# Twelve names in other places of a hand-written attention schedule

## The chip, the cores and the metric

The kernel runs on one core of a Trainium2 chip. The metric is the device time of one execution in microseconds. The tensors are fp32; matrix products are made of three matmuls on split operands (a high part, rounded to the matmul's input format, and a low part, the rest).

## The reference

Two transformer layers over 1024 tokens of width 1024, each a token mixer and a gated MLP with a causal depthwise convolution. Layer 0's mixer, the part that the change touches, is differential attention: 8 heads, each with two sets of queries and keys of 64 columns, one value of 128 columns, and a chunk-causal mask.

```python
def diff_attention(h, w_qkv, ..., subln_g, w_o, lambda_init, cos, sin):
    qkv = h @ w_qkv
    ...                                  # rotary on the first 16 of 64 columns of q and k
    def block(args):                     # 128 queries at a time
        sc = jnp.einsum('bqhcd,bkhcd->bhcqk', qb, k).astype(jnp.float32) * scale
        p = masked_softmax(sc, chunk_mask(blk, s)[None, None, None])
        a = p[:, :, 0] - lam * p[:, :, 1]
        return jnp.einsum('bhqk,bkhe->bqhe', a.astype(v.dtype), v)
    ...
    o = rms_norm(o, subln_g) * (1.0 - lambda_init)
    return o.reshape(b, s, D_MODEL) @ w_o
```

Layer 1 (multi-head latent attention) and the two MLPs are as large in time, but nothing of theirs changes.

## The kernel before, in words

Layer 0's attention is cut into 32 steps: 8 heads with 4 steps each, step p of a head (p = 0 to 3) for the query blocks 2p and 2p+1 of 128 tokens, with the keys up to there. A step is a bundle of small named parts (`DaStep`), and each part issues one or a few instructions on one engine. Beside the steps run the projections of what comes next: `units` gives each step one or two of them (U, V), again in named parts.

The order of all this is written out by hand. `DA_SCORE` has four rows, one for each p; row t mod 4 is read when step t is current. A name without a mark belongs to step t, each `'` means one step earlier, each `+` one later. `da_steps` reads a row from left to right and calls the parts; a name of a step or a part that does not exist is skipped. The engines TensorE, VectorE, ScalarE and GpSimd run what they are given in exactly this order, each in its own queue; two names on different engines are ordered only by their data, by buffers that come free, and by nothing in the row. The DMA queue of SP is not under the manual order. Row t = 1 is replaced by `DA_SECOND`, and the last four steps (t = 28 and on) by `DA_END`.

The names, with the engine and the line by which the profile shows them:

- S0, S1: scores of the step's two blocks (TensorE, 1914 and 1915). M0, M1: mask and row maximum (VectorE, 1924 and 1925; 1928 and 1929 for p above 1, where a and b mark the two components). E0a, E0b, E1a, E1b: exponentials (ScalarE, 1940).
- I0, I1: inverse of the row sums (VectorE, 1945 and 1946). C0, C1: scaling of the first component by it (line 149 on GpSimd for p below 2, line 147 on ScalarE else). X0, X1: the mixing, first component plus a negative multiple of the second (VectorE, 1953).
- T0 to T3: transposes of the mixed probabilities (TensorE, 1961), three or four of 128x128 each. H0 to H3: high part (ScalarE, 127). L0 to L3: low part (VectorE, 130). A0 to A3: product with the values (TensorE, 119 to 121). O: copy of the product (ScalarE, 1989).
- Q1, Q2 (ScalarE, 1995 and 1998), Q3 (GpSimd, 130), F (TensorE, 2006 and 2007), R1 to R3 (ScalarE, 2013 to 2017), N1 to N3 (VectorE, 2022 to 2026): squares, their sum, and the head's normalisation, ending in a store. They exist for odd p.
- U0, U1, V0, V1: the two halves of a projection, 12 matmuls each (TensorE, 119 to 121, into the one bank `u`). Us, Um (VectorE, 657 and 661) and Up, Ua (GpSimd, 689): rotary. Uka to Ukd: keys, where a and c are casts of ScalarE (672) and b and d low parts of VectorE (670). Uqa to Uqf: queries, where a, b, d, e are casts of ScalarE (127) and c and f low parts of GpSimd (130). Vc, Vt, Vh, Vl: values (ScalarE 640, TensorE 645, ScalarE 127, VectorE 130).
- Wh, Wl: high and low part of the next head's weights, 128x1024 (ScalarE, 127; GpSimd, 130). Wl also starts the load of the next weights.

Step 3 of a head keeps TensorE busy into the next head: its probabilities are transposed and multiplied in rows 0 and 1 (T0', A0', then T3'', A1'', A2'', A3''), and the sum of squares F'' follows in row 1.

Of the kernel before, what the change touches and what calls it, by code (L numbers as in the profile page):

```python
# [56 lines left out]
class Trunk:  # L57
# [234 lines left out]
    def steps(self, attend, units, prepare, n, apart=False):  # L292
# [32 lines left out]


    DA_SCORE = (
# [4 lines left out]
    )  # L332

    DA_SECOND = "S0 I1' Vc' Ukd' H2'' M0 L2'' A1'' C0' X0' H3'' E0b L3'' U0 A2'' E0a Wh Vt' N3'''' A3'' O'' Wl' Q2'' C1' I0 X1' U1 C0 S1 X0 Us Vh' Q1'' T0' H0' Q3'' Up F'' Um M1 Ua Wl R1'' Vl' E1b V0 E1a L0' I1 A0' Uqa R2'' R3'' Uqd Uqe Uqb C1 X1 N1'' Uqc V1 T1 T0 Uqf H0"

    DA_END = (
# [9 lines left out]
    def da_steps(self, attend, units, prepare, n, extra):  # L346
# [4 lines left out]
        with self.tc.manual_schedule(engines={E.PE, E.DVE, E.Activation, E.Pool}):  # L351
            for t in range(-1, first + len(self.DA_END)):
                while len(steps) < min(n, t + 2):
# [3 lines left out]
                    for name, u in zip("UV", units(x)):  # L357
                        steps[x].parts.update({name + part: f for part, f in u.items()})
                row = self.DA_SECOND if t == 1 else self.DA_SCORE[t % 4] if t < first else self.DA_END[t - first]
                for name in row.split():  # L360
# [2004 lines left out]
```

## Time and profile before

| what | value |
|---|---|
| runs, median (lowest to highest) | 2399.78 us (2396.99 to 2400.72) |
| profiled execution | 2396.82 us, its span 2395.0 us |
| TensorE matmul busy | 2348.3 us (98%) |
| VectorE busy | 1947.0 us (81%) |
| ScalarE busy | 1292.0 us (54%) |
| GpSimd busy | 613.6 us (26%) |
| mean granted TensorE clock | 0.998 |
| layer 0's attention in rows and ending | about 48 us to 480 us |

The span is the time from the first to the last instruction. Busy shares are means over stages with different limits; what a change in one stage is worth is read from that stage: which engine TensorE waits for there, and what that engine was waiting for. Times in the timeline count from the start of the span.

### The profile page before, as it was taken

What the parts mean: (1) busy time and instruction counts of PE and PEld (TensorE: products, weight loads), DVE (VectorE), ACT (ScalarE), POOL (GpSimd) and SP (SyncE); (2) the same over time, 40 slices, a digit from 0 to 9 for tenths busy, and PEclk for the clock granted to TensorE, in tenths of its full rate; (3) what the DMA queues carried; (4) which work ended last, traced back from release to release, by engine and by line L of the source; (5) the groups of instructions that cost most, each with busy time, mean ns of one, the idle gap of its engine ahead of it and who ended that gap; (6) DMA issues with size and microseconds to landing.
All of it is one profiled execution on the core that took longest, in us unless ns stands there. A gap on an engine that the chain in (4) does not pass through costs nothing.

```text
span 2395.0 us, 32652 instructions
## 1 busy us (share of the span) xinstructions
PE 2348.3 (98%) x11952; PEld 1995.3 (83%) x11952; DVE 1947.0 (81%) x3185; ACT 1292.0 (54%) x2367; POOL 613.6 (26%) x484
## 2 busy tenths in 40 slices
PE   8999999999999999999999999999999999999998
PEld 7888888888888888888898789988888888887886
DVE  7888888858888888999864788886488888889997
ACT  5677767745444444443445777775354444444544
POOL 4555555424000000000132666664320000000001
PEclk9999999999999999999999999999999999999999
DMA  3111111333222222643222111123322222227502
GB/s 146 40 36 36 36 49 54 111 101 115 80 86 91 80 80 83 229 167 99 82 91 64 60 41 41 41 87 114 107 79 83 92 81 79 82 86 281 176 1 79
DMA packets 95664, 213.39 MB, mean 89 GB/s; under 512 B 8712, under 2 KB 33936, under 8 KB 95504
## 3 DMA queue, kind: packets, MB, share of 16 engines
q1 hardware_dynamic: 86304, 183.51, 23.0%
q10 hardware_dynamic: 9200, 27.80, 3.1%
q8 instruction: 94, 1.54, 0.3%
q14 instruction: 66, 0.54, 0.1%
HBM read 158.85 MB, written 52.43 MB: 88 GB/s over the span
## 4 chain that ended last, share of the span: by engine, by line
PE 85%; DVE 6%; ACT 3%; issue 2%; DMA 2%; POOL 2%; SPq 0%; POOLq 0%; DVEq 0%; ACTq 0%
PE S L119 13%; PE S L121 13%; PE S L120 13%; PE b L119 8%; PE b L120 8%; PE b L121 8%; PE u L119 4%; PE u L121 4%; PE u L120 4%; PE b L263 2%; PE u L2071 1%; PE u L2070 1%; PE S L1915 1%; PE S L1914 1%; PE b L1961 1%
## 5 line engine op out<-in xcount | busy, mean ns | idle before, releaser
L167 POOL TENSOR_TENSOR st<-st,mhalf 128x1 f32<-128x1 f32 x56 | 36.2, 647 | 1307.9 <-DVE st L164 1300.0
L119 PE MATMUL S<-s,u 128*128 128x512 f32 (+1 forms) x800 | 302.1, 378 | 2.5 <-DVE s L130 2.1
L121 PE MATMUL S<-s,u 128*128 128x512 f32 (+1 forms) x800 | 301.1, 376 | 0.4 <-DVE u L130 0.4
L120 PE MATMUL S<-s,u 128*128 128x512 f32 (+1 forms) x800 | 301.0, 376 | 0.0
L127 ACT CAST u<-h 128x512 fp32r<-128x512 f32 (+2 forms) x242 | 145.6, 619 | 273.3 <-DVE h L1082 271.6
L119 PE MATMUL b<-s,u 128*128 128x512 f32 x588 | 230.7, 392 | 1.8 <-DVE u L130 1.3
L121 PE MATMUL b<-s,u 128*128 128x512 f32 x588 | 229.0, 389 | 0.0
L120 PE MATMUL b<-s,u 128*128 128x512 f32 x588 | 229.0, 389 | 0.0
L1139 DVE SCALAR_TENSOR_TENSOR u<-u,conv,u 128x1023 f32<-128x1023 f32 (+1 forms) x176 | 224.9, 1278 | 0.8 <-ACT u L1135 0.7
L149 POOL TENSOR_TENSOR u<-u,st 128x512 f32<-128x512 f32 (+7 forms) x160 | 172.5, 1088 | 167.8 <-DVE st L2056 103.3
L127 ACT CAST s<-u 128x512 fp32r<-128x512 f32 (+3 forms) x230 | 145.4, 665 | 94.7 <-PE u L121 27.1
L119 PEld LDWEIGHTS S<-s,u 128*128 128x128 f32 x800 | 150.5, 188 | 30.9 <-DVE s L130 2.7
L130 DVE TENSOR_TENSOR u<-b,u 128x512 fp32r<-128x512 f32 (+1 forms) x256 | 158.6, 631 | 20.8 <-ACT u L127 18.2
L121 PEld LDWEIGHTS S<-s,u 128*128 128x128 f32 x800 | 150.5, 188 | 28.1 <-DVE u L130 0.6
L120 PEld LDWEIGHTS S<-s,u 128*128 128x128 f32 x800 | 150.5, 188 | 27.4
L127 ACT CAST u<-b 128x512 fp32r<-128x512 f32 (+1 forms) x256 | 134.9, 546 | 71.1 <-PE b L1961 39.7
L119 PE MATMUL u<-s,s 128*128 128x512 f32 (+1 forms) x408 | 162.4, 398 | 2.2 <-DVE s L130 1.3
L121 PE MATMUL u<-s,s 128*128 128x512 f32 (+1 forms) x408 | 157.9, 387 | 0.0
L120 PE MATMUL u<-s,s 128*128 128x512 f32 (+1 forms) x408 | 157.7, 387 | 0.0
L130 DVE TENSOR_TENSOR s<-u,s 128x512 fp32r<-128x512 f32 (+2 forms) x204 | 139.0, 715 | 11.8 <-ACT s L127 11.4
L1142 ACT ACTIVATE u<-u 128x1024 f32<-128x1024 f32 x44 | 46.7, 1062 | 186.5 <-DVE u L1139 186.4
L130 DVE TENSOR_TENSOR u<-h,u 128x512 fp32r<-128x512 f32 x171 | 117.4, 687 | 32.5 <-ACT u L127 31.5
(290 smaller groups left out, 6538.0 us busy)
## 6 DMA issues: line engine op xcount, KB each, us to landing
u<-in_ffn_up SPq DMA_DIRECT2D x88, 512.0 KB, 3.8
g_d<-u ACTq DMA_DIRECT2D x44, 512.0 KB, 2.6
u<-in_ffn_down SPq DMA_DIRECT2D x66, 256.0 KB, 4.7
u<-g_d SPq DMA_DIRECT2D x62, 256.0 KB, 4.2
s<-in_da_wqkv SPq DMA_DIRECT2D x23, 512.0 KB, 3.6
x_d<-u SPq DMA_DIRECT2D x16, 512.0 KB, 3.0
s<-x_d SPq DMA_DIRECT2D x8, 1024.0 KB, 10.4
u<-o_d SPq DMA_DIRECT2D x24, 256.0 KB, 2.9
```

Source lines behind the costliest of these rows:

```text
L119: mm(out, lh, rl, start=first, stop=False, skip_group_check=onto)
L120: mm(out, lh, rh, start=False, stop=False, skip_group_check=onto)
L121: mm(out, ll, rh, start=False, stop=last, skip_group_check=onto)
L127: self.nc.scalar.copy(out, src)
L130: (eng or self.nc.vector).tensor_sub(out, src, hi.bitcast(F32))
L149: self.nc.gpsimd.tensor_mul(x, x, s.to_broadcast(list(x.shape)))
L167: nc.gpsimd.tensor_tensor(r, s, self.mhalf, ALU.pow)
L263: self.nc.tensor.transpose(ps[:, j * P : (j + 1) * P], probs[t][:, k : k + P], self.ident)
L1139: nc.vector.scalar_tensor_tensor(t[half][:, back:], u[half][:, : S - back], w, t[half][:, back:], ALU.mult, ALU.add)
L1142: nc.scalar.activation(t[0], t[0], AF.Silu)
L1914: nc.tensor.matmul(sc[c][:, b : b + m], ql[c][:, qs], kt[:, c, :m], start=True, stop=False)
L1915: nc.tensor.matmul(sc[c][:, b : b + m], qh[:, c, qs], kt[:, c, :m], start=False, stop=True)
```

## The change

It is a change of four strings; no function changes, and no instruction is added or taken out. Moved are, in row 0: V0 behind R3''', T2' behind E0b, and T3' out of the row. In row 1 (and in `DA_SECOND`): T3'' near the front, Wh before U0, C1' before O'' (so before Wl'), X1' behind Wl', and Uqa behind R3''. In row 3: Uqb' before X1', and R1'' before I1.

```diff
     DA_SCORE = (
-        "S0 S1 M0 Up O'' R2''' V0 X1' R3''' N1''' M1 T1' Ua E0a H1' L1' Uka E1a T0' H0' T2' Ukb Ukc V1 E0b L0' I0 E1b A0' N2''' T3'",
-        "S0 I1' Vc' Ukd' H2'' M0 L2'' A1'' C0' X0' H3'' E0b L3'' U0 A2'' E0a Wh Vt' N3'''' A3'' O'' Wl' Q2'' C1' I0 X1' U1 C0 S1 X0 Us Vh' Wl Q1'' T0' H0' Q3'' Up F'' Um M1 Ua R1'' Vl' E1b V0 E1a L0' I1 A0' Uqa R2'' R3'' Uqd Uqe Uqb C1 X1 N1'' Uqc V1 T1 T0 Uqf H0",
+        "S0 S1 M0 Up O'' R2''' X1' R3''' V0 N1''' M1 T1' Ua E0a H1' L1' Uka E1a T0' H0' Ukb V1 Ukc E0b T2' L0' I0 E1b A0' N2'''",
+        "S0 I1' Vc' Ukd' T3'' H2'' M0 L2'' A1'' C0' X0' H3'' E0b L3'' Wh U0 A2'' E0a Vt' N3'''' A3'' C1' O'' Wl' X1' Q2'' I0 U1 C0 S1 X0 Us Vh' Wl Q1'' T0' H0' Q3'' Up F'' Um M1 Ua R1'' Vl' E1b V0 E1a L0' I1 A0' R2'' R3'' Uqa Uqd Uqe Uqb C1 X1 N1'' Uqc V1 T1 T0 Uqf H0",
         ...
-        "S0 U1 X1' Uqb' M0b T2' T0' Q2'' Q1'' ... Ul E1b I1 R1'' C1 +Um A2'",
+        "S0 U1 Uqb' X1' M0b T2' T0' Q2'' Q1'' ... Ul E1b R1'' I1 C1 +Um A2'",
     )
```

`DA_SECOND` gets the same edits as row 1.

More of the change, by code (lines that the diff above doesn't have):

```diff
@@ L327 @@
     DA_SCORE = (
[2 rows of a table removed]
[2 rows of a table added]
         "S0 Vm' O'' Vs' M0a L0' U0 Vp' Wh M0b E0a E0b Va' A0' I0 U1 N2''' H1' L1' Vka' Wl N3''' Vkc' Us Um C0 S1 M1b M1a E1b A1' E1a Vkd' Up +U0 Vkb' Ua I1 Uqa Uqd C1 Uqf Uqe O' X0",
[1 row of a table removed]
[1 row of a table added]
     )
-    DA_SECOND = "S0 I1' Vc' Ukd' H2'' M0 L2'' A1'' C0' X0' H3'' E0b L3'' U0 A2'' E0a Wh Vt' N3'''' A3'' O'' Wl' Q2'' C1' I0 X1' U1 C0 S1 X0 Us Vh' Q1'' T0' H0' Q3'' Up F'' Um M1 Ua Wl R1'' Vl' E1b V0 E1a L0' I1 A0' Uqa R2'' R3'' Uqd Uqe Uqb C1 X1 N1'' Uqc V1 T1 T0 Uqf H0"
+    DA_SECOND = "S0 I1' Vc' Ukd' T3'' H2'' M0 L2'' A1'' C0' X0' H3'' E0b L3'' Wh U0 A2'' E0a Vt' N3'''' A3'' C1' O'' Wl' X1' Q2'' I0 U1 C0 S1 X0 Us Vh' Q1'' T0' H0' Q3'' Up F'' Um M1 Ua Wl R1'' Vl' E1b V0 E1a L0' I1 A0' R2'' R3'' Uqa Uqd Uqe Uqb C1 X1 N1'' Uqc V1 T1 T0 Uqf H0"
     DA_END = (
```

2 rows, old and new, of the table DA_SCORE are left out of this document.

## The prediction

> **What bounds the kernel now.** I read the page first, for its chain of waits.
>
> ```profile
> PE 85%; DVE 6%; ACT 3%; issue 2%; DMA 2%; POOL 2%; SPq 0%; POOLq 0%; DVEq 0%; ACTq 0%
> ```
>
> TensorE carries 85% of the chain that ends last, so an edit to the order of names can only win the time in which TensorE stands still, or lose by making it stand longer. Next I read TensorE's waits, for the stretch in which the edited rows 0 and 1 run in their steady form (84 to 412 us, heads 1 to 6).
>
> ```profile
> PE b L2006 <- POOL h L130: 2.6, 6, 0.4
> PE b L119 <- DVE u L130: 1.9, 6, 0.4
> ```
>
> Two waits, once per head each, and no other: F'' (line 2006, released by GpSimd's Q3'') and A2'' (line 119, released by VectorE's L2''). Both stand in row 1. The first head's rows skip the names of steps that do not exist (no A2'', no F''), and the last head runs the untouched ending, so the change acts six times.
>
> The timeline of head 1 shows what the waits cost. Its columns are start, duration, instruction, and in brackets the idle time with its releaser. TensorE:
>
> ```profile
> 106.40 0.49 PE L1961 MATMUL b<-ident,u 128*128 128x128 f32 x3
> 106.65 0.42 PE L1914 MATMUL S<-u,h 128*128 128x384 f32 x1
> ...
> 110.43 0.39 PE L120 MATMUL u<-s,s 128*128 128x512 f32 x1
> 110.66 0.39 PE L121 MATMUL u<-s,s 128*128 128x512 f32 x1
> 111.41 0.39 PE L119 MATMUL b<-u,u 128*128 128x256 f32 x1 [0.36 <-DVE u L130]
> ...
> 117.04 0.49 PE L1961 MATMUL b<-ident,u 128*128 128x128 f32 x3
> 117.94 0.50 PE L2006 MATMUL b<-h,ones 128*128 128x512 f32 x1 [0.41 <-POOL h L130]
> ...
> 125.92 0.40 PE L1914 MATMUL S<-u,h 128*128 128x512 f32 x1
> ```
>
> The idle time in brackets is less than what is lost, as a matmul's reported end lies behind the next one's start. Matmuls of 512 columns follow each other after 0.23 (110.43 to 110.66), so A2'' was due at 110.89 and came at 111.41: 0.52 lost. Three transposes are followed by the next work after 0.25 (106.40 to 106.65), so F'' was due at 117.29 and came at 117.94: 0.65 lost. Together 1.17 us per head, 7.0 us over six: no more can be won.
>
> Why do L2'' and Q3'' come late? GpSimd and VectorE:
>
> ```profile
> 105.70 0.40 POOL L149 TENSOR_TENSOR u<-u,st 128x128 f32<-128x128 f32 x1 [5.72 <-DVE st L1945]
> 106.06 2.85 POOL L130 TENSOR_TENSOR s<-s,s 128x1024 fp32r<-128x1024 f32 x1
> 108.86 1.07 POOL L149 TENSOR_TENSOR u<-u,st 128x256 f32<-128x256 f32 x1
> 112.96 0.83 POOL L149 TENSOR_TENSOR u<-u,st 128x384 f32<-128x384 f32 x1 [3.03 <-PE b L645]
> 113.75 2.58 POOL L130 TENSOR_TENSOR s<-s,s 128x1024 fp32r<-128x1024 f32 x1
> 116.29 1.59 POOL L130 TENSOR_TENSOR h<-h,h 128x512 fp32r<-128x512 f32 x1
> ...
> 122.25 3.00 POOL L130 TENSOR_TENSOR h<-h,u 64x512 fp32r<-64x512 f32 x2
> ...
> 129.04 2.40 POOL L130 TENSOR_TENSOR s<-s,s 128x1024 fp32r<-128x1024 f32 x1
> ```
>
> These are, in order, C0', Wl', C1', C0, Wl, Q3'', then Uqc with Uqf, and a Wl of row 2.
>
> ```profile
> 103.60 0.68 DVE L670 SCALAR_TENSOR_TENSOR u<-h,u 64x512 fp32r<-64x512 f32 x1
> ...
> 106.57 0.15 DVE L1945 RECIPROCAL st<-st 128x2 f32<-128x2 f32 x1
> ...
> 106.99 2.47 DVE L670 SCALAR_TENSOR_TENSOR u<-h,u 64x512 fp32r<-64x512 f32 x1
> 109.48 0.17 DVE L1924 MEMSET S<- 64x128 f32 x1
> ...
> 110.67 0.69 DVE L130 TENSOR_TENSOR u<-b,u 128x512 fp32r<-128x512 f32 x1
> 111.28 0.34 DVE L1953 SCALAR_TENSOR_TENSOR u<-u,st 128x128 f32<-128x128 f32 x1
> 111.54 0.55 DVE L130 TENSOR_TENSOR u<-b,u 128x384 fp32r<-128x384 f32 x1
> 112.00 0.74 DVE L2026 SCALAR_TENSOR_TENSOR h<-h,g_sub,h 128x512 f32<-128x512 f32 x1
> 112.66 0.15 DVE L1945 RECIPROCAL st<-st 128x2 f32<-128x2 f32 x1
> ...
> 112.98 1.08 DVE L1953 SCALAR_TENSOR_TENSOR u<-u,st 128x256 f32<-128x256 f32 x1
> ```
>
> These are Ukb', I1' (its reciprocal), Ukd', M0, L2'', X0', L3'', N3'''', I0 and X1'. The key is line 670: the same instruction on the same shape took 0.68 at 103.60 and 2.47 at 106.99, and the 2.47 began while Wl' ran. It ended at 109.46, so its own 0.68 began at 108.78, just when Wl' (to 108.91) let go. A VectorE instruction with two inputs in SBUF and a GpSimd instruction exclude each other; I call what they share the port. So Wl', which nobody needs until V0 behind F'', holds up Ukd', and behind it in VectorE's order M0, L2'' and I0; I0 starts C0, and C0, Wl, Q3'' follow each other on GpSimd up to F''.
>
> **The change, part by part.** On each engine only these orders change: TensorE runs V1 before T2', and S0 of row 1 before T3'; GpSimd runs C1' before Wl'; VectorE runs X1' before I0; ScalarE runs Wh before E0a, and R2'', R3'' before Uqa. V0 and X1' in row 0, and Uqb' with X1' and R1'' with I1 in row 3, pass only names of other engines, so no queue changes: zero. No instruction is added or removed. The weight load that Wl' starts on SP's queue moves with it by some 1.5 us; it is first read in row 2, a whole row later. ScalarE's rows:
>
> ```profile
> 106.37 0.59 ACT L127 CAST u<-b 128x512 fp32r<-128x512 f32 x1
> ...
> 110.67 0.58 ACT L1940 ACTIVATE u<-S,st 128x384 f32<-128x384 f32 x1 [1.85 <-DVE st L1925]
> ...
> 111.80 1.04 ACT L127 CAST s<-s 128x1024 fp32r<-128x1024 f32 x1
> ...
> 120.80 0.61 ACT L127 CAST u<-h 64x512 fp32r<-64x512 f32 x1
> 121.31 0.64 ACT L2015 ACTIVATE h<-h 128x512 f32<-128x512 f32 x1
> ...
> 122.63 1.90 ACT L127 CAST u<-h 64x512 fp32r<-64x512 f32 x3
> ```
>
> (H2'', E0b, Wh, Uqa, R2'', and Uqd, Uqe, Uqb.)
>
> *Transposes: zero.* T2' now stands before A0' instead of before V1. A0' is six matmuls that end where T3' starts, 106.40; they have at most 256 columns, half of what takes 0.23, so about 0.12 each and 0.7 in all (an estimate), and T2' is done at 105.7 to 105.9. H2'', its reader, starts at 106.37 behind other work of ScalarE: about 0.5 us of cover. T3' goes behind S0 and so 0.78 later at most; H3'' waits for A1'' anyway, whose position is the same. If the cover were gone, the price would be the transposes' own 0.3 to 0.4.
>
> *C1' before Wl': the gain.* I0's reciprocal at 112.66 released C0 at 112.96, 0.30 later; so I1' (106.57) releases C1' at 106.87. It has 256 columns: between C0' (0.40 for 128) and C0 (0.83 for 384), 0.62, to 107.49. The port is free 0.13 before GpSimd's reported end (108.78 against 108.91), so Ukd' runs from 107.36, with 0.70 to the next instruction, to 108.06; before, 109.46. M0 takes 1.19 to its follower (109.48 to 110.67): 109.25. L2'' takes 0.61: 109.86. A2'', due at 110.89, waits no more: 0.52 won.
>
> Wl' gets the port at 108.06. With the port, it takes 2.27 (Wl after X1': 112.98 + 1.08 = 114.06 to 113.75 + 2.58 = 116.33): to 110.33, port free at 110.20. X0' waits from 109.86 until then, and with the spacings of before (0.26, 0.46, 0.66) L3'' starts at 110.46, N3'''' at 110.92 and X1' at 111.58.
>
> *X1' before I0* puts about 0.35 ahead of I0 (X0', half as wide, is 0.26 from its follower): I0 at 111.93, against 112.66: 0.73 earlier. *Wh before E0a*: M0's end at 109.25 starts E0b, 0.57; Wh, about 0.95 to its follower; E0a with its accumulator read 0.8: done at 111.6, 0.3 before I0's turn, so free. Without this cover it would put up to 0.95 into I0.
>
> C0 then ends at 113.06. Before, X1' took the port between C0 and Wl, so that Wl lasted 2.58; now Wl takes the 2.40 seen at 129.04: 0.18 more. F'' comes 0.91 earlier if X0 follows Wl as now. If X0 slips in ahead of Wl, that costs about 0.12: 0.79. Middle: **0.85 us per head**. F'' at 117.09, with TensorE ready at 117.29 - 0.52 = 116.77: a wait of 0.3 stays.
>
> *R2'', R3'' before Uqa: no cost, but a thinner cover.* They put about 1.3 (121.31 to 122.63) ahead of Uqa, which itself moves up by some 0.7 with VectorE's and TensorE's earlier work: Uqa at 121.4, done at 122.0. Uqc starts there, after X1 has used the port; the two took 3.00 with X1's turn of some 0.5 between them, so Uqf ends 2.5 to 2.7 later, at 124.7 instead of 125.25. Its reader, the second component of S0, comes at 125.92 - 0.85 = 125.07. The spare falls from 0.67 to 0.35. Bounds: 0 to 0.3 us per head.
>
> **Sum.** Six times 0.85 is 5.1 us. The profiled execution took 2396.8 us, 1.8 over its span of 2395.0; with the change 2391.7. The runs' median, 2399.8, lies 3.0 above the profiled one, so I forecast **2394.7 us**. Bounds per head: 0.5, if X1' and the port eat a third of it and Uqf another 0.1, to 1.17: 2396.8 to 2392.8. A measurement of this kernel can tell about 0.2% (4.8 us) from no change, so my point stands right at that line.
>
> **Rivals.** *Slower: the port stays with GpSimd.* When C1' ends, Ukd' waits for the port and Wl' stands next in GpSimd's queue. If Wl' takes it, Ukd' waits for both: 107.45 + 2.40 = 109.85, to 110.5 instead of 109.46, 1.0 later; with X1' ahead of I0 0.35 more, less the 0.18: F'' comes 1.2 later, six times, 7.2 us: 2407. It decides where Wl' starts within 0.1 us of C1' and before Ukd'. [...] Against this stands the trace: X1' asked at 112.98 while C0 ran to 113.79 with Wl right behind it, and X1' was done at 114.06, before Wl. VectorE got the port between two GpSimd instructions without a gap.
>
> *Nothing measurable: the waits move.* If F'' gains only what A2'' does, or S0 of row 2 starts to wait for Uqf (the thin cover), 0.2 to 0.5 per head stay: 2396.8 to 2398.6. For it speaks that four edits lie on the same chain of three engines; against it, that each has 0.3 us of room.
>
> **Chances.** Forecast's case 0.70, of which 0.48 beyond 0.2% and 0.22 within (its bounds reach from 3.0 to 7.0 us, and the line is at 4.8); moved waits 0.12, all within 0.2%; slower 0.18, the port's rival and what else an order this tight can upset. So faster 0.48, same 0.34, slower 0.18. The range takes in the forecast's bounds and the moved waits, and 1.5 to 2.5 us of the spread of runs (2397.0 to 2400.7): 2391.2 to 2401.0; the port's rival is left out.
>
> **What would show it.** Right: line 670's second instruction of row 1 under 1.3 us instead of 2.47; no wait at A2''; F'' still released by GpSimd, but 0.57 after the three transposes start (117.09 less 116.52) instead of 0.90. Wrong: line 670 still above 2.4, S0 of row 2 waiting for GpSimd, or the wait at F'' above 0.5.

## The result and the profile after

| | before | after |
|---|---|---|
| median of 7 runs (lowest to highest) | 2397.86 us (2396.99 to 2400.72) | 2391.25 us (2389.19 to 2392.87) |
| ratio, 95% interval | | 0.9971 [0.9962, 0.998] |
| profiled execution, its span | 2396.82 us, 2395.0 us | 2391.42 us, 2389.6 us |

The kernel got faster by 0.29%. The page after, engines' busy time and the chain that ended last:

```profile
PE 2347.6 (98%) x11952; PEld 1995.9 (84%) x11952; DVE 1930.0 (81%) x3185; ACT 1291.3 (54%) x2367; POOL 610.9 (26%) x484
...
PE 87%; DVE 6%; ACT 2%; DMA 2%; issue 1%; POOL 1%; SPq 0%; POOLq 0%; DVEq 0%; ACTq 0%
```

The instruction counts are those of before, but VectorE is busy for 17.0 us less; 10.6 of them are line 670's (33.2 us in its 30 instructions before, 22.6 after), whose waits stand in the trace as busy time: Ukd' took 2.47 where the same instruction took 0.68 at 103.60. TensorE's waits between 84 and 412 us are an empty list; the two entries of before (A2'' and F'', 4.5 us together) are gone. For the size of the gain I use mainly one measure: the time from F'' in row 3 to F'' in row 1 of the next head. F'' (the first, of line 2006) of row 3 before:

```profile
96.82 0.40 PE L2006 MATMUL b<-h,ones 128*128 128x512 f32 x1
```

to 117.94 is 21.12 us. TensorE after, same head:

```profile
96.52 0.40 PE L2006 MATMUL b<-h,ones 128*128 128x512 f32 x1
...
111.18 0.28 PE L121 MATMUL b<-u,u 128*128 128x256 f32 x1
111.30 0.60 PE L645 MATMUL b<-ident,h 128*128 128x128 f32 x4
...
116.11 0.49 PE L1961 MATMUL b<-ident,u 128*128 128x128 f32 x3
116.63 0.50 PE L2006 MATMUL b<-h,ones 128*128 128x512 f32 x1
```

That is 20.11 us, **1.01 less**; in the heads 1 to 6 it is 20.10 to 20.13, against 21.10 to 21.13. A whole head, from F'' in row 1 to F'' in the next head's row 1, takes 54.83 against 55.82, so rows 2 and 3 give nothing of it back. The matmuls of A2'' now run on without a bracket up to Vt' (line 645, 111.30). F'' follows the three transposes after 0.52 instead of 0.90; free of any wait it would be 0.25, so 0.27 is still lost. VectorE and GpSimd after:

```profile
103.30 0.69 DVE L670 SCALAR_TENSOR_TENSOR u<-h,u 64x512 fp32r<-64x512 f32 x1
...
106.68 0.97 DVE L670 SCALAR_TENSOR_TENSOR u<-h,u 64x512 fp32r<-64x512 f32 x1
...
108.87 0.69 DVE L130 TENSOR_TENSOR u<-b,u 128x512 fp32r<-128x512 f32 x1
...
111.12 0.47 DVE L1953 SCALAR_TENSOR_TENSOR u<-u,st 128x256 f32<-128x256 f32 x1
111.52 0.15 DVE L1945 RECIPROCAL st<-st 128x2 f32<-128x2 f32 x1
...
112.68 2.74 DVE L1953 SCALAR_TENSOR_TENSOR u<-u,st 128x384 f32<-128x384 f32 x1 [0.76 <-POOL u L149]
```

```profile
106.50 0.62 POOL L149 TENSOR_TENSOR u<-u,st 128x256 f32<-128x256 f32 x1 [0.70 <-DVE st L1945]
107.07 2.86 POOL L130 TENSOR_TENSOR s<-s,s 128x1024 fp32r<-128x1024 f32 x1
111.81 0.83 POOL L149 TENSOR_TENSOR u<-u,st 128x384 f32<-128x384 f32 x1 [1.89 <-DVE st L1945]
112.60 2.41 POOL L130 TENSOR_TENSOR s<-s,s 128x1024 fp32r<-128x1024 f32 x1
114.97 1.61 POOL L130 TENSOR_TENSOR h<-h,h 128x512 fp32r<-128x512 f32 x1
...
121.42 2.92 POOL L130 TENSOR_TENSOR h<-h,u 64x512 fp32r<-64x512 f32 x2 [0.39 <-ACT u L127]
```

Ukd' (line 670, 106.68) takes 0.97 where it took 2.47: it waits only for C1' (106.50 to 107.12), and Wl' (107.07, 2.86 long where Wl at 112.60 took 2.41) waits for it. Six heads at 1.00 give 6.0 us, and 0.3 came before head 1, where two executions of one kernel differ by more than that (last section); the span fell by 5.4. So about 1 us was given back, and it was given back in the ending. There TensorE stands still twice, at the last T0' and at F'', in both kernels; after:

```profile
447.22 0.69 PE L1961 MATMUL b<-ident,u 128*128 128x128 f32 x2 [1.65 <-DVE u L1953]
448.43 0.80 PE L2006 MATMUL b<-h,ones 128*128 128x512 f32 x1 [0.52 <-POOL h L130]
```

The windows from the end of that stall to the ending's second F'', before and then after (columns: stretch, its length, busy time and count of TensorE, weight loads, VectorE, ScalarE, GpSimd, then the granted clock, DMA share, GB/s):

```profile
453.40:482.68 29.28, 28.45 (x149) 24.39 (x149) 23.66 (x45) 22.11 (x42) 10.69 (x9) 0.94 0.21 66
```

```profile
447.20:477.43 30.23, 29.69 (x148) 25.46 (x149) 23.64 (x44) 22.07 (x42) 10.64 (x9) 0.89 0.20 61
```

The same work takes 1.0 us longer at a mean granted clock (the share of TensorE's full clock) of 0.89 instead of 0.94. The stretch of low clock in it, before and then after:

```profile
455.00:458.41 3.41, 3.41 (x12) 2.81 (x11) 2.60 (x4) 2.55 (x6) 2.21 (x3) 0.50 0.02 5
```

```profile
447.20:454.05 6.85, 6.31 (x20) 5.23 (x21) 4.15 (x9) 5.29 (x11) 5.52 (x5) 0.50 0.18 47
```

The clock is at one half for 3.41 us before and for 6.83 us after (447.22 to 454.05 by the trace's clock record), and full in the rest of the stretch.

### The profile page after: what moved, and what is told of

The parts are those of the page before. It is cut to its first block, busy times and chain, and to the rows that moved or that the text cites. A ratio compares the mean times of both kernels' runs of the same rounds, so it can differ in the third digit from the quotient of the medians.

```text
span 2389.6 us, 32651 instructions
## 1 busy us (share of the span) xinstructions
PE 2347.6 (98%) x11952; PEld 1995.9 (84%) x11952; DVE 1930.0 (81%) x3185; ACT 1291.3 (54%) x2367; POOL 610.9 (26%) x484
## 4 chain that ended last, share of the span: by engine, by line
PE 87%; DVE 6%; ACT 2%; DMA 2%; issue 1%; POOL 1%; SPq 0%; POOLq 0%; DVEq 0%; ACTq 0%
PE S L119 13%; PE S L121 13%; PE S L120 13%; PE b L119 8%; PE b L120 8%; PE b L121 8%; PE u L119 4%; PE u L121 4%; PE u L120 4%; PE b L263 2%; PE u L2071 1%; PE u L2070 1%; PE S L1915 1%; PE S L1914 1%; PE b L1961 1%
```

## The experiments

My theory is the prediction's: Wl' holds the port that Ukd' needs (2.47 us beside Wl', 0.68 with GpSimd idle), Ukd' holds up everything behind it on VectorE, and only "C1' ahead of Wl'" matters. Rivals: the gain is that C1' itself comes early; or it needs several of the moves. Counted by the diff, the moves are ten, not twelve: V0, T2', V1, T3, Wh, C1', X1', Uqa, Uqb' and R1'', five of them once more in `DA_SECOND`. Up to the table below, each total is one execution, beside one of the kernel before on the same chip; the distance per head, nearly the same in every head, is the surer number.

**C1' ahead of Wl', alone** (the kernel before with one name moved, in row 1 and `DA_SECOND`).

```diff
- N3'''' A3'' O'' Wl' Q2'' C1' I0 X1' U1
+ N3'''' A3'' C1' O'' Wl' Q2'' I0 X1' U1
```

> The kernel before, with one edit alone: C1' ahead of Wl' on GpSimd (rows 1 and its twin for the first head). Measured is the distance from the start of the sum F'' in row 3 to that of the next one in row 1 (line 2006): 21.11 us before, 20.11 after, the same in six heads. Port theory (Wl' held up VectorE's Ukd'): this edit carries the gain; Ukd' takes under 1.3 us instead of 2.47, the wait at A2'' is gone, the distance is 20.0 to 20.2, the time 5 to 6 us below before. Rival, the gain comes from the order on VectorE and ScalarE (X1' ahead of I0, Wh ahead of E0a): Ukd' is faster, but F'' is not, and the distance stays above 20.5. Rival, it comes from the transposes' places on TensorE: 21.1.

19.90 to 19.91 us in five of six heads (20.18 in the first), no wait of TensorE left, 2391.75 us against 2396.08. Head 2, VectorE and TensorE:

```profile
162.96 0.98 DVE L670 SCALAR_TENSOR_TENSOR u<-h,u 64x512 fp32r<-64x512 f32 x1
```

```profile
172.43 0.49 PE L1961 MATMUL b<-ident,u 128*128 128x128 f32 x3
172.71 0.50 PE L2006 MATMUL b<-h,ones 128*128 128x512 f32 x1
```

F'' follows the transposes after 0.28: one edit of ten brings all, and 0.2 us per head more than the whole change. The other nine together cost. The total does not show this (2391.75 here, 2391.42 in the profile after): in this execution the first F'' of all came 1.40 us later (97.92), and the ending took 29.92 us instead of 29.00.

**The transposes' moves, alone** (T2' behind E0b, T3' into row 1, V1 ahead of Ukc).

```diff
- T0' H0' T2' Ukb Ukc V1 E0b L0' I0 E1b A0' N2''' T3'
+ T0' H0' Ukb V1 Ukc E0b T2' L0' I0 E1b A0' N2'''
- S0 I1' Vc' Ukd' H2'' M0
+ S0 I1' Vc' Ukd' T3'' H2'' M0
```

> The kernel before, with T2' behind V1 and T3' behind the next row's S0, nothing else. Port theory: no effect, distance 21.1 (within 0.05), both waits of TensorE as before; H2'' still starts behind ScalarE's other work. Transposes rival: 20.1 to 20.5.

21.11 to 21.12 us, 2396.46 us, and TensorE's waits as before:

```profile
PE b L2006 <- POOL h L130: 2.7, 6, 0.4
PE b L119 <- DVE u L130: 2.2, 6, 0.4
```

**X1' ahead of I0, with C1' still behind Wl'.**

```diff
- O'' Wl' Q2'' C1' I0 X1' U1
+ O'' Wl' C1' X1' Q2'' I0 U1
```

> The kernel before, with X1' ahead of I0 on VectorE (C1' stays behind Wl'), nothing else. Port theory: I0 comes 0.4 later, Wl loses the 0.18 for which X1' held it; F'' comes 0.1 to 0.3 later, distance 21.2 to 21.4, Ukd' stays at 2.47. Rival, the VectorE order gives the gain: 20.6 or less.

21.32 us, 0.21 more; 2399.34 us. TensorE's waits:

```profile
PE b L2006 <- POOL h L130: 3.9, 6, 0.7
```

**Wh ahead of U0, E0a and A2'', in the kernel before.**

```diff
- L3'' U0 A2'' E0a Wh Vt'
+ L3'' Wh U0 A2'' E0a Vt'
```

> The kernel before, with Wh ahead of E0a on ScalarE, nothing else. Port theory: without the earlier M0 there is no room for it; E0a ends near 113.0 on the first such head's clock of before, I0 waits for it, distance 21.4 to 21.6, so 2 to 3 us slower in all. Rival, the ScalarE order gives part of the gain: below 21.1.

21.33 to 21.36 us, 0.23 more, a little under the expected bottom; 2400.78 us:

```profile
PE b L2006 <- POOL h L130: 4.0, 6, 0.7
```

**The kernel after, with Wl' back ahead of C1'.**

```diff
- A3'' C1' O'' Wl' X1' Q2'' I0 U1
+ A3'' O'' Wl' C1' X1' Q2'' I0 U1
```

> Kernel after, with Wl' put back ahead of C1' and X1' still ahead of I0: the exact reverse of the edit that gained alone. Measure: the distance from F'' in row 3 to F'' in row 1 of the same head, 20.11 us in the kernel after, 21.11 before. Port theory: Ukd' takes 2.4 to 2.5 us again, TensorE waits again at A2'' and F'', and I0 behind X1' costs its 0.2 on top: 21.2 to 21.4, total 2397 to 2399. Rival (the gain needs the other moves of the change too, or comes from where X1' stands): 20.1 to 20.6.

21.31 to 21.34 us, 2400.13 us against 2397.26 (0.21 in each of six heads, and an ending of 30.03 us where the profile before has 28.01): without its one good edit the change would gain nothing. Ukd' is back at its 2.47, and the waits are back:

```profile
163.08 2.47 DVE L670 SCALAR_TENSOR_TENSOR u<-h,u 64x512 fp32r<-64x512 f32 x1
```

```profile
PE b L2006 <- POOL h L130: 3.9, 6, 0.7
PE b L119 <- DVE u L130: 2.2, 6, 0.4
```

The rival "needs several moves" falls.

**The kernel after, with X1' back behind I0.**

```diff
- C1' O'' Wl' X1' Q2'' I0 U1
+ C1' O'' Wl' Q2'' I0 X1' U1
```

> Kernel after, with X1' back behind I0 and C1' still ahead of Wl'. Theory: the 0.2 us per head by which the whole change is behind its own edit of C1' come from I0 standing behind X1' on VectorE, which starts C0, Wl and Q3'' on GpSimd later: 19.9 to 20.0, and total 2390 to 2391.5. Rival (they come from Wh ahead of U0, or from the late transposes): 20.1 as in the kernel after.

19.89 to 19.90 us, so X1' ahead of I0 costs 0.21 per head in this order too. It still holds all the other moves, Wh ahead of E0a and the transposes' among them, and is as fast per head as C1' first alone; so these are free once C1' stands first, while Wh alone cost 0.23 in the kernel before, where Ukd' delays M0 and with it E0a. The total was 2392.15 us all the same: the first F'' of all came at 97.98 us (96.52 in the profile after), and the ending took 29.86 us (29.00). What lies outside the six heads moves by as much as the edit is worth.

**Every Wl in two halves, in the old place.** This separates the port from C1': by the theory the port comes free in the middle of Wl', while C1' still waits for all of it.

```diff
- self.lo(st.w[:, 1, :], st.raw, st.w[:, 0, :], nc.gpsimd)
+ for s in (slice(0, 512), slice(512, 1024)):
+     self.lo(st.w[:, 1, s], st.raw[:, s], st.w[:, 0, s], nc.gpsimd)
```

> Kernel before, with every Wl made as two instructions of 512 columns instead of one of 1024, in its old place ahead of C1'. Port theory: Ukd' gets the port between the two halves and ends 1.2 to 1.4 us earlier (1.0 to 1.3 us long instead of 2.47), so the wait at A2'' goes and about 0.5 of the 1.0 us per head is had: 20.5 to 20.7; the second half keeps C1' as late as before. Rival (what counts is only that C1' stands behind 2.85 us of Wl'): 21.0 to 21.3, since C1' comes no earlier.

20.16 to 20.17 us, no wait in TensorE's list, 2392.60 us against 2397.26. VectorE and GpSimd (the added line moves the line numbers by one):

```profile
161.84 1.36 DVE L671 SCALAR_TENSOR_TENSOR u<-h,u 64x512 fp32r<-64x512 f32 x1
```

```profile
160.55 0.40 POOL L149 TENSOR_TENSOR u<-u,st 128x128 f32<-128x128 f32 x1 [5.68 <-DVE st L1946]
160.91 3.44 POOL L130 TENSOR_TENSOR s<-s,s 128x512 fp32r<-128x512 f32 x2
164.31 0.61 POOL L149 TENSOR_TENSOR u<-u,st 128x256 f32<-128x256 f32 x1
```

Ukd' got the port between the halves, as the theory said, at 1.36 us (the first half ended at 162.64, Ukd' at 163.20, the second half at 164.35); C1' began 3.76 after C0', later than before (108.86 - 105.70 = 3.16). Yet 0.95 of the 1.0 us came. So C1' being early is worth nothing by itself; that rival falls. My own number, half of the gain, was wrong too: I took the waits at A2'' and F'' for two effects, of which the halves would cure the first. Both are one delay: Ukd' ended 1.1 earlier, and so did I0, which starts the chain to F''.

**Wl' of row 1 in row 0, where GpSimd is idle** (the kernel before with one name moved; C1' stays).

```diff
- V0 X1' R3''' N1''' M1 T1' Ua E0a H1'
+ V0 X1' R3''' N1''' M1 T1' Ua Wl E0a H1'
- A3'' O'' Wl' Q2'' C1' I0
+ A3'' O'' Q2'' C1' I0
```

> Kernel before, with the low part Wl' of row 1 taken to row 0, behind Ua, where GpSimd is idle; C1' stays behind O''. Port theory: nothing of GpSimd stands against Ukd' in row 1, so Ukd' takes 0.7 us, both waits go: 19.8 to 20.0, total 2390 to 2391.5. Rival (the port is as dear in row 0: 2.85 us of GpSimd now stand against two-input instructions of VectorE there and delay TensorE): 20.5 or more.

19.87 us in every head, 2390.25 us against 2397.26. GpSimd, VectorE and TensorE of head 2:

```profile
155.27 3.36 POOL L130 TENSOR_TENSOR s<-s,s 128x1024 fp32r<-128x1024 f32 x1
```

```profile
162.12 0.61 POOL L149 TENSOR_TENSOR u<-u,st 128x256 f32<-128x256 f32 x1 [0.70 <-DVE st L1945]
```

```profile
162.30 0.97 DVE L670 SCALAR_TENSOR_TENSOR u<-h,u 64x512 fp32r<-64x512 f32 x1
```

```profile
171.77 0.49 PE L1961 MATMUL b<-ident,u 128*128 128x128 f32 x3
172.02 0.48 PE L2006 MATMUL b<-h,ones 128*128 128x512 f32 x1
```

F'' follows after 0.25, the unhindered distance. Ukd' took 0.97 and not the expected 0.7, as C1' (162.12) began just ahead of it. In row 0 Wl took 3.36 instead of 2.85, beside a mixing of 1024 columns on VectorE (154.64, 1.75 long, as at 99.31 in the kernel before), but TensorE waits for neither: its list of waits is empty. From F'' to F'' this edit seemed the best; a whole head takes 54.66 us, though, just as with C1' first (54.66), since rows 2 and 3 lose about 0.08 here. It was timed, with the kernel after beside it on the same chip:

> The kernel before with only Wl' moved to row 0, timed. Port theory: 1.24 us in each of six heads, 7.4 us in all, with the place of the low clock in the ending adding up to 2 us either way: ratio 0.9965 to 0.9975 to the kernel before. Rival (the whole change keeps something that this edit lacks): no better than the whole change, 0.9971 or above.

> The whole change again, beside the other two: 2391 to 2392 us, ratio 0.997; 20.11 us from F'' in row 3 to F'' in row 1. If the two others are faster by over 1 us here, the order of the whole change is not the best use of its one effective edit.

| same chip | median (lowest to highest) | ratio to before, 95% interval |
|---|---|---|
| before, 10 runs | 2397.57 us (2394.89 to 2399.38) | |
| the whole change, 7 runs | 2389.85 us (2388.99 to 2391.93) | 0.9968 [0.9957, 0.998] |
| Wl' in row 0 alone, 5 runs | 2388.55 us (2388.32 to 2388.92) | 0.9962 [0.9949, 0.9976] |

The slowest run of Wl' in row 0 (2388.92) lies just below the fastest of the whole change (2388.99), and the medians differ by 1.3 us, where 0.17 per whole head makes 1.0; the intervals against the kernel before overlap. Both kernels came out faster than expected (ratio 0.9965 to 0.9975, and 2391 to 2392 us): of the 9.0 us of Wl' in row 0 six whole heads at 1.16 explain 7.0, and the rest is not assigned. In this profile of the kernel after the heads again took 20.10 to 20.12 us, but the ending 28.00 instead of 29.00, and the first F'' came at 98.00 instead of 96.52: one kernel, two executions.

**Is it the stall that lowers the clock in the ending?** The kernel with Wl' in row 0, and products that nobody uses on TensorE in the two stalls:

```diff
+ if name == "spin":
+     ps = self.bank("u")
+     for _ in range(13 if spun == 0 else 5):
+         nc.tensor.matmul(ps[:, :P], self.ones, self.ones, start=True, stop=True)
...
- Q3'' Uqb Uqd T0' H0' Uqf F'' E0b
+ Q3'' Uqb Uqd spin T0' H0' Uqf spin F'' E0b
```

> Kernel before with Wl' in row 0 (as measured alone: 19.87 us per head, total 2390.25), and in addition 13 and 5 products of ones by ones on TensorE, in a bank that nobody reads, where it stands still in the ending: ahead of the three transposes that wait for the mixing X (a stall of 1.63 us), and ahead of F'' (0.78 us). They compute nothing that is used. Clock theory: the granted clock falls to one half behind this stall because TensorE stood still; with the stall filled it stays at full speed, the stretch from the last head's F'' to the ending's (28.06 us with 3.41 us at half speed, 30.0 with 6.83) falls to 26 to 27, total 2386 to 2389. Rival (the clock falls for another reason, or the stall is too short to matter): the low clock stays at this place, 28 to 30 us, total 2390 to 2392.

TensorE (line numbers moved by six), and the windows of the same stretch, which starts with the added products:

```profile
444.28 1.62 PE L366 MATMUL u<-ones 128*128 128x128 f32 x13
445.73 0.29 PE L1967 MATMUL b<-ident,u 128*128 128x128 f32 x1
446.23 0.44 PE L1967 MATMUL b<-ident,u 128*128 128x128 f32 x2 [0.21 <-DVE u L1959]
446.43 0.76 PE L366 MATMUL u<-ones 128*128 128x128 f32 x5
447.44 0.50 PE L2012 MATMUL b<-h,ones 128*128 128x512 f32 x1 [0.25 <-POOL h L130]
```

```profile
444.20:474.71 30.51, 29.86 (x170) 25.27 (x169) 26.04 (x48) 24.00 (x46) 12.03 (x10) 1.00 0.23 72
```

The granted clock stays at 1.00; in all twelve other profiles, which have the stalls, it drops to half there. From F'' to F'' the ending took 27.27 us, against 28.06 and 28.01 in the two profiles of the row-0 kernel, both with the short low stretch, and 29.00 to 30.04 in the six profiles with the long one. The expected 26 to 27 was too low: I had charged the low clock with half its length, but the short stretch of 3.41 us cost under 0.8. That other engines set the pace for part of it is likely, not shown. The median, 2387.70 us (2386.17 to 2389.66; ratio 0.9959 [0.9945, 0.9973]), is 0.85 under the row-0 kernel's, with ranges that overlap: the clock's part is shown by the trace, in one profile; the total's is not settled.

## Why the prediction was right or wrong

*The mechanism held.* The second line 670 of row 1 took 0.97 us (forecast: under 1.3), A2'' waits no more, and F'' is still held back after the transposes, by 0.52 (forecast 0.57). Measured from the head's start (0.30 earlier than before), the steps came so: L2'' at 109.17 (forecast 109.25), X1' at 111.42 (111.58), I0 at 111.82 (111.93), F'' at 116.93 (117.09). X0 waits behind Wl (112.68, 2.74 long), and Wl took 2.41 (forecast 2.40).

*The per-head term was mis-sized: 1.00 us instead of 0.85.* Two pieces make it. I took the middle between "X0 follows Wl" (0.91) and "X0 slips in" (0.79), although nothing had changed in who asks first; the trace shows the first. And C1' began at 106.80 in before's time, not 106.87, with everything behind it on that lead. Both sizes are small, 0.9 us over six heads.

*The ending was left out.* I said that the last head runs the untouched ending and put it at zero. Its instructions are untouched, but its time is not fixed: the low clock at its stalls lasted 3.41 or 6.83 us in the profiles, worth 1.0 us between the kernels before and after. That took back what the per-head term had been short of, which is why the forecast for the profiled execution, 2391.7, sits so near the measured 2391.42. The agreement is partly luck.

*The step that failed is the baseline.* I put the median 3.0 us above the profiled execution, as three runs had it; over seven runs it was 1.0 above (2397.86 against 2396.82), and after the change it was 0.2 below (2391.25 against 2391.42). The forecast of 2394.7 is 3.4 too high: 1.9 because the median of before was 2397.86 and not 2399.8, and 1.5 because the fall from median to median was 6.6 and not 5.1. Of that 1.5, 0.9 is the per-head term above; for the other 0.6 no run shows a cause. So the forecast lay 0.13% under the median of before where 0.29% was measured: the point lay inside what I had called no change, and the result outside it. The range (from 2391.2) just held it. The seven runs of before spread over 3.7 us, and executions of one kernel differ by about 1 us in each of two places: the first F'' of all came at 96.42 and 97.50 in two of the row-0 kernel, and the ending of the kernel after took 29.00 and 28.00.

*The rivals.* The slower case, that the port stays with GpSimd, did not come: Wl' was next in GpSimd's queue when C1' ended (107.12), and Ukd' went first (done at 107.65, Wl' at 109.93). How long Ukd' took went with what ran beside it: 2.47 beside Wl' of 1024 columns, 1.36 beside one of 512, 0.97 beside C1', and 0.68 to 0.69 for the same instruction with GpSimd idle (103.60 before, 103.30 after). L2'', one of whose inputs lies in a bank of PSUM, took 0.69 beside Wl' (108.87 after) and 0.69 for the same form with GpSimd idle (104.03). In these places a VectorE instruction already waiting got its turn between two GpSimd instructions: Ukd' between C1' and Wl' after, and in the kernel before X1' (112.98 to 114.06) between C0 (to 113.79) and Wl (to 116.33). The moved waits did not come either: Uqc and Uqf end at 121.42 + 2.92 = 124.34, and their reader starts here:

```profile
124.62 0.40 PE L1914 MATMUL S<-u,h 128*128 128x512 f32 x1
```

0.28 of spare, against the forecast 0.35. *Transposes: zero* and *Wh: free* held, Wh only with C1' first. *X1' before I0* was charged with 0.35 in I0's time and cost 0.21 in F''; I counted it inside the gain and did not say that the change would be better without it.

## What to carry to other kernels

When the same instruction on the same shape has two durations in a trace, look for what ran beside it on another engine (here 0.68 with GpSimd idle, 2.47 beside Wl'): the cure here was to move or split the long instruction that nobody waits for, and the gain was everything queued behind the one that waited. Of a bundle of reorderings, price each alone: here one of ten carried it all, and another cost a fifth of it. A distance inside the trace must also cover what comes behind it: 0.08 us of the best distance here was lost in the next rows. Where a change is worth 0.2 to 0.3%, measure it by a distance inside the trace that repeats per head, and take the median for the baseline from more than three runs.

## What the runs showed of the hardware

- A stall of 1.6 us on TensorE, with 0.5 to 0.8 right behind it, goes with half the granted clock for 3.41 or 6.83 us (twelve profiles of twelve; 0.94 and 0.89 over some 30 us), and with the stalls filled by unused products it does not (1.00, one profile). In the 3.41 us up to the fall (451.59 to 455.00 and 443.81 to 447.22) TensorE stood still for 2.4 us before and for 2.0 us after (0.35 and 1.65), where the fall came ahead of the second stall.
- Which of the two lengths an execution gets does not follow the kernel: the kernel after had 29.00 us in its ending once and 28.00 another time. By the trace's clock record the fall came 440.32 us behind the first full clock in the one and 433.49 in the other, 6.83 apart. What decides between the two lengths is not shown. A second stretch of half clock lies near 1330 us in the profiles before (3.41 us from 1335.64) and after (6.83 us from 1324.45), far behind the edited rows.
- The start differs from one execution to the next as well. Matmuls of one shape, equally long behind the start of the span, in the two profiles of the kernel after, the first and the later one:

```profile
15.18 0.28 PE L119 MATMUL u<-s,s 128*128 128x256 f32 x1
15.29 0.28 PE L120 MATMUL u<-s,s 128*128 128x256 f32 x1
```

```profile
15.18 0.41 PE L120 MATMUL u<-s,s 128*128 128x256 f32 x1
15.39 0.41 PE L121 MATMUL u<-s,s 128*128 128x256 f32 x1
```

  One follows the other after 0.11 in the first, where the clock record has full clock from 6.91 us on, and after 0.21 in the second, where it has it from 16.33 on; the second's first F'' comes 1.48 later. A median of three runs does not settle an offset of 2 us.
